# Attention projections emitted one group ahead of the scores, across pairs of heads

## The chip, the cores and the metric

The kernel runs on one core of a Trainium2 chip. The metric is device time in microseconds (us) of one execution, as the median of several runs. Engines are named PE or TensorE (matrix products), DVE or VectorE, ACT or ScalarE, POOL or GpSimd, and SP or SyncE, which here does nothing but issue DMA transfers from one queue, in order.

## What is computed

A trunk of two layers over 1024 tokens of width 1024: a state-space mixer with a feed-forward network, then dilated attention with a second feed-forward network. The change touches the attention only. Cut to what matters, for three groups with dilation 1, 4 and 16 and 16 heads of 64 each:

```python
q = (h @ w_q) * (HEAD_DIM ** -0.5)
for g, (_, dil) in enumerate(DILATED_GROUPS):
    kb, vb = kv_blocks[2 * g], kv_blocks[2 * g + 1]
    qb = _to_residue_blocks(q[:, :, g], dil)
    s = einsum('brnqhe,brnkhe->brnhqk', qb, kb) + bias
    s = where(valid, s, NEG_BIG)
    lse = logsumexp(s)
    p = exp(s - lse)
    outs.append(einsum('brnhqk,brnkhe->brnqhe', p, vb)); lses.append(lse)
wts = softmax(stack(lses), axis=0)
o = einsum('gblh,gblhe->blhe', wts, stack(outs))
return o @ w_out
```

The three groups of a head are merged by one softmax over their sums, so a head's output can begin only when the scores of all three groups are there.

## The kernel before

Products with weights are done in three passes of a split number: a weight tile `raw` (512 KB) is loaded, ScalarE casts it to a high part `wh` (L83), VectorE subtracts for the low part `wl` (L84), and TensorE multiplies `wh`, `wl` with both parts of the activations `hT` (L88 to L90, 24 matmuls for 512 tokens).

The attention works on eight pairs of heads. `values` come first for all heads and are stored to memory. For each pair and each of the groups 0, 1 and 2, `Pair.proj(g)` projects queries and keys: four tiles `qk` of 24 matmuls (two halves of the tokens for queries, two for keys). Each tile is evacuated from PSUM as `qh` (ScalarE, L632 or L635) and `ql` (VectorE, L633 or L636), and small transfers (128 KB, L644 to L647) move them into the stacked tiles `qs` and `kl`, apart for the two heads. `Pair.scores(g)` multiplies queries and keys (L695), VectorE adds the bias tile `bt` and takes the maximum (L683, two instructions), and ScalarE takes exponentials of group 0 (L714). The bias tile of a pair is loaded when the Pair is made (L660, L662). `Pair.output()` loads the values `V` (L810), takes the exponentials of groups 1 and 2 (L740), merges the groups by `softmax()` (two exchange matmuls `x`, L755, each fed by VectorE's `bd`, L750), transposes the weights (`t`, copied to `pt`) and multiplies them with `V` into `o` (L832); VectorE adds the second half of it to `oT` (L876), which is stored as `oscr` (L883).

The pools hold two weight sets, two `raw` tiles, two PSUM banks for `qk`, four for scores, transposes and exchanges together, four `qh`/`ql` tiles, two `V` tiles, one `bt`, and ten `q` tiles for `qs` and `kl`. A group's queries and keys for both heads take six `q` tiles, so group 1's last two tiles (those of the second head's keys) take places that group 0 leaves when its first head is scored.

The kernel doesn't write the order of an engine's instructions. The program's text gives each instruction a priority, and a list scheduler places them by a timing model of its own, with the tiles' dependencies and free buffers. So the emission order shifts priorities, and an engine's queue need not follow it. SyncE's queue gets its transfers in the order that the scheduler fixes, and each waits in it for its own buffers and data.

Of the kernel before, what the change touches and what calls it, by code (L numbers as in the profile page):

```python
# [28 lines left out]
class Pool:  # L29


    def __init__(self, net, pool, bufs):
        self.net, self.pool, self.bufs = net, pool, bufs
# [489 lines left out]
def skew(scr, h0, q0, qstep, nq):  # L523

    ap = scr[:]
    off = ap.offset + h0 * P * LB + q0 * (LB - 1) + 127
    return bass.AP(ap.tensor, off, [[qstep * (LB - 1), nq], [P * LB, 2], [1, 256]])
# [14 lines left out]
def value_tile(net, blk, j, hT, ws, ps, st):  # L542

    nc, g = net.nc, blk // 2
    hf = tile_half(g, j)
    for k in range(KT):
        x = hT[k][hf]
        cols = tok_cols(x, g, j)
        wh, wl = (w[:, (k % 2) * 512 : (k % 2) * 512 + 512] for w in ws[k // 2])
        net.mm3(ps, x[:, 0, cols], x[:, 1, cols], wh, wl, k == 0, k == KT - 1)  # L550
    (nc.scalar.copy if j % 2 else nc.vector.tensor_copy)(st.rearrange("p a b -> p (a b)"), ps)
    h0 = 4 * (blk % 2)
    nc.sync.dma_start(net.vscr[g, h0 : h0 + 4, :, j, :].rearrange("h p c -> p h c"), st)
# [13 lines left out]
def attention(net, hT, ap, ws):  # L567
    nc = net.nc
    net.evn = 0
    for blk in range(2 * NG):  # L570
        if blk:
            ws = [net.wload(net.a["w_v"][blk, i], **({"pool": ap, "tag": "q"} if i < 3 else {})) for i in range(4)]
        else:
            ws = ws + [net.wload(net.a["w_v"][0, i], pool=ap, tag="q") for i in (2, 3)]
        for j in range(8) if blk else range(4, 8):
            ps = net.psA.tile([P, 512], F32, "mm", "v")
            st = ap.tile([P, 4, P], F32, "pt", "vs")
            value_tile(net, blk, j, hT, ws, ps[:], st[:])

    net.oscr = net.dp.tile([8, P, T], F32, name="oscr")  # L580
    nxt = Pair(net, 0, hT, ap)
    nxt.proj(0)
    for hp in range(8):
        pair = nxt
        for g in range(NG):
            if g:
                pair.proj(g)
            pair.scores(g)
        if hp < 7:
            nxt = Pair(net, hp + 1, hT, ap)  # L590
            nxt.proj(0)
        oT = pair.output()

    row = [[net.xp.tile([P, 2, 512], F32R, "x", "gT") for k in range(KT)] for _ in range(2)]
    for k in range(KT):
        if k < 7:
            raw = net.rawp.tile([P, T], F32, "raw", "oraw")
            nc.sync.dma_start(raw[:], net.oscr[k])
        else:
            raw = oT  # L600
        for hf in range(2):
            x = row[hf][k]
            net.split(raw[:, hf * 512 : hf * 512 + 512], x[:, 0, :], x[:, 1, :], nc.gpsimd if k < 7 else nc.vector)
    return [[row[hf][k] for hf in range(2)] for k in range(KT)]
# [46 lines left out]
class Pair:  # L651


    def __init__(self, net, hp, hT, ap):
        nc = net.nc
        self.net, self.hp, self.hT, self.ap = net, hp, hT, ap
        self.qk = {}
        self.bt = ap.tile([P, NG, 2, 256], F32, "bt", "bt")
        for r in range(4):
            nc.sync.dma_start(self.bt[32 * r : 32 * r + 32, 0], skew(net.bscr[0], 2 * hp, r, 4, 32))  # L660
        for g in (1, 2):
            nc.sync.dma_start(self.bt[:, g], skew(net.bscr[g], 2 * hp, 0, 1, P))  # L662
# [858 lines left out]
def program(tc, a, out):  # L1521
    nc = tc.nc
    with ExitStack() as ctx:
# [16 lines left out]
        for l in range(2):  # L1540
            if l == 1:
                with ExitStack() as c:
                    gT = attention(net, hT, setup(net, c), V0)
# [113 lines left out]
```

## Time and profile before

| | |
|---|---|
| time, median of 3 runs | 3102.1 us (3097.02 to 3108.28) |
| the profiled execution's own time | 3093.69 us |
| its span, first to last instruction | 3091.9 us |
| TensorE busy | 2885.9 us (93% of the span) |
| VectorE busy | 1900.4 us (61%) |
| ScalarE busy | 1115.8 us (36%) |
| chain that ended last, share of TensorE | 77% |
| mean granted TensorE clock | 0.962 of full speed |

The profile is one execution. The scores and outputs of the attention lie between about 1400 and 2270 us of the span, and from about 1540 on they repeat with one head pair to a period. Busy shares are means over stages, so the rows further down are taken from this stage alone. A row of a timeline ends, where the engine had been idle, with the idle time in brackets and the operation that ended it.

### The profile page before, as it was taken

How to read it: one execution, taken by the hardware profiler on the slowest of the kernel's cores; microseconds unless marked ns; L12 is line 12 of the kernel's file. 1: busy time of each engine (PE TensorE's matmuls, PEld its weight loads, DVE VectorE, ACT ScalarE, POOL GpSimd, SP SyncE). 2: the span in 40 equal slices, each digit the busy share in tenths (PEclk: the TensorE clock that was granted, in tenths of full speed). 3: DMA queues.
4: the chain of work that ended last, by engine and by line, in shares of the span. 5: the costliest groups of instructions: out<-in, count | busy, mean ns of one | idle time of the engine just before them, and what ended most of it. 6: DMA issues, size and time to landing. Idle time of an engine off the chain costs nothing.

```text
span 3091.9 us, 37869 instructions
## 1 busy us (share of the span) xinstructions
PE 2885.9 (93%) x13926; PEld 2365.8 (77%) x13926; DVE 1900.4 (61%) x3517; ACT 1115.8 (36%) x1939; POOL 260.3 (8%) x259
## 2 busy tenths in 40 slices
PE   3689989999999989999999999999689899999998
PEld 3668768888788868998777777778567688887886
DVE  8964689888666651113544445354457988886577
ACT  2433344444333331103443334343423544443232
POOL 7930000000100000000000000000250000001000
PEclk8889989999999999999999999999799999999999
DMA  5231523333563333326565456456435232336432
GB/s 179 59 119 61 171 86 125 109 109 108 183 255 111 115 121 99 108 72 164 148 153 144 133 133 178 119 150 157 123 141 172 87 123 104 109 106 257 162 134 91
DMA packets 187016, 408.03 MB, mean 132 GB/s; under 512 B 22480, under 2 KB 64192, under 8 KB 186832
## 3 DMA queue, kind: packets, MB, share of 16 engines
q1 hardware_dynamic: 178384, 373.11, 39.0%
q0 software_dynamic: 8448, 32.51, 2.9%
q8 instruction: 110, 1.80, 0.3%
q14 instruction: 74, 0.61, 0.1%
HBM read 249.75 MB, written 89.73 MB: 110 GB/s over the span
## 4 chain that ended last, share of the span: by engine, by line
PE 77%; DVE 6%; issue 6%; POOL 4%; DMA 4%; ACT 2%; SPq 1%; DVEq 0%; POOLq 0%; ACTq 0%
PE dn L412 10%; PE p L89 8%; PE p L90 8%; PE p L88 8%; PE qk L88 6%; PE qk L89 6%; PE qk L90 6%; PE o L832 3%; PE v L88 3%; PE v L90 3%; PE v L89 3%; PE t L822 2%; PE s L695 2%; PE pa L89 1%; PE pa L88 1%
## 5 line engine op out<-in xcount | busy, mean ns | idle before, releaser
L84 DVE TENSOR_TENSOR wl<-raw,wh 128x1024 fp32r<-128x1024 f32 x174 | 222.8, 1281 | 274.3 <-ACT wh L83 270.2
L412 PE MATMUL dn<-wh,ax 128*128 128x512 f32 x1408 | 381.6, 392 | 6.5 <-DVE yv L333 3.9
L88 PE MATMUL p<-xc,wc 128*128 128x512 f32 x880 | 352.1, 401 | 14.2 <-ACT wc L83 14.2
L83 ACT CAST wh<-raw 128x1024 fp32r<-128x1024 f32 x174 | 182.6, 1050 | 495.4 <-PE qk L89 160.5
L89 PE MATMUL p<-xc,wc 128*128 128x512 f32 x880 | 352.2, 400 | 0.0
L90 PE MATMUL p<-xc,wc 128*128 128x512 f32 x880 | 347.9, 400 | 2.7 <-DVE wc L84 2.7
L88 PE MATMUL qk<-hT,wh 128*128 128x512 f32 x768 | 308.9, 402 | 10.4 <-DVE ql L633 10.4
L412 PEld LDWEIGHTS dn<-wh,ax 128*128 128x128 f32 x1408 | 265.7, 189 | 64.2 <-DVE yv L333 4.7
L89 PE MATMUL qk<-hT,wh 128*128 128x512 f32 x768 | 308.7, 402 | 0.0
L90 PE MATMUL qk<-hT,wl 128*128 128x512 f32 x768 | 307.3, 400 | 0.0
L412 PE MATMUL dn<-wl,ax 128*128 128x512 f32 x704 | 218.8, 392 | 0.1
L88 PEld LDWEIGHTS p<-xc,wc 128*128 128x128 f32 x880 | 167.9, 191 | 58.8 <-ACT wc L83 19.2
L90 PEld LDWEIGHTS p<-xc,wc 128*128 128x128 f32 x880 | 167.3, 190 | 44.7 <-DVE wc L84 5.0
L89 PEld LDWEIGHTS p<-xc,wc 128*128 128x128 f32 x880 | 168.0, 191 | 39.4
L83 ACT CAST wc<-s 128x512 fp32r<-128x512 f32 x176 | 107.6, 620 | 239.9 <-PE p L90 158.6
L401 DVE TENSOR_TENSOR wl<-wd,wh 128x1024 fp32r<-128x1024 f32 x88 | 112.8, 1285 | 119.1 <-ACT wh L397 119.0
L88 PEld LDWEIGHTS qk<-hT,wh 128*128 128x128 f32 x768 | 148.0, 193 | 41.8 <-DVE ql L633 12.4
L397 ACT CAST wh<-wd 128x1024 fp32r<-128x1024 f32 x88 | 91.8, 1049 | 228.8 <-PE dn L412 107.8
L90 PEld LDWEIGHTS qk<-hT,wl 128*128 128x128 f32 x768 | 147.9, 193 | 29.7
L89 PEld LDWEIGHTS qk<-hT,wh 128*128 128x128 f32 x768 | 148.1, 193 | 29.0
L88 PE MATMUL v<-wh,hT 128*128 128x512 f32 x384 | 153.7, 401 | 6.7 <-DVE tmp L183 5.5
L683 DVE CUSTOM_DVE_ANT_0 p<-s,bt 128x256 f32<-128x256 f32 (+1 forms) x384 | 119.1, 370 | 65.4 <-PE s L695 64.7
(296 smaller groups left out, 5706.3 us busy)
## 6 DMA issues: line engine op xcount, KB each, us to landing
raw<-in_w_up SPq DMA_DIRECT2D x94, 512.0 KB, 3.6
vs<-cv SPq DMA_DIRECT2D x88, 512.0 KB, 3.0
vs<-vs SPq DMA_DIRECT2D x88, 512.0 KB, 6.3
qs<-qh SPq DMA_DIRECT2D x288, 128.0 KB, 2.4
raw<-in_w_out SPq DMA_DIRECT2D x48, 512.0 KB, 3.5
kl<-ql SPq DMA_DIRECT2D x192, 128.0 KB, 2.4
wd<-in_w_down POOLq DMA_DIRECT2D x44, 512.0 KB, 15.3
raw<-in_w_v SPq DMA_DIRECT2D x26, 512.0 KB, 3.6
```

What stands on the lines that cost most here:

```text
L83: nc.scalar.copy(hi, x)
L84: (eng or nc.vector).tensor_tensor(out=lo, in0=x, in1=hi.bitcast(F32), op=ALU.subtract)
L88: nc.tensor.matmul(out, lh, rh, start=first, stop=False)
L89: nc.tensor.matmul(out, lh, rl, start=False, stop=False)
L90: nc.tensor.matmul(out, ll, rh, start=False, stop=last)
L397: nc.scalar.copy(w[0][:], raw)
L401: nc.vector.tensor_tensor(out=w[1][:], in0=raw, in1=w[0][:].bitcast(F32), op=ALU.subtract)
L412: nc.tensor.matmul(ps[i][h][:], l_, w[wi][:, h * 512 : h * 512 + 512], start=(f == 0 and l_ is ah and wi == 0), stop=(f == NF - 1 and l_ i ...
L683: nc.vector.tensor_tensor_reduce(out=out, in0=s, in1=b, scale=1.0, scalar=-3.0e38, op0=ALU.add, op1=ALU.max, accum_out=m)
L695: nc.tensor.matmul(out, qx[:, qs], kv[i], start=(i == 0), stop=(i == 1))
L822: nc.tensor.transpose(ps[:, i * P : i * P + P], b, net.ident[:])
L832: nc.tensor.matmul(o[64 * h : 64 * h + 64, oc], v[:, 64 * h : 64 * h + 64], pt[h], start=st, stop=sp_)
```

## The change

In the text of the program, the projection of a group is emitted before the scores of the group ahead of it, and the first projection of the next pair before the last scores of this one. For that the load of the bias tile leaves the constructor: it becomes `load_bias()`, called for the next pair after the scores of group 2, since there is one bias tile.

```diff
--- before.py
+++ after.py
@@ -578,17 +578,21 @@
             value_tile(net, blk, j, hT, ws, ps[:], st[:])
 
     net.oscr = net.dp.tile([8, P, T], F32, name="oscr")
+
     nxt = Pair(net, 0, hT, ap)
+    nxt.load_bias()
     nxt.proj(0)
     for hp in range(8):
         pair = nxt
         for g in range(NG):
-            if g:
-                pair.proj(g)
+            if g < 2:
+                pair.proj(g + 1)
+            elif hp < 7:
+                nxt = Pair(net, hp + 1, hT, ap)
+                nxt.proj(0)
             pair.scores(g)
         if hp < 7:
-            nxt = Pair(net, hp + 1, hT, ap)
-            nxt.proj(0)
+            nxt.load_bias()
         oT = pair.output()
 
     row = [[net.xp.tile([P, 2, 512], F32R, "x", "gT") for k in range(KT)] for _ in range(2)]
@@ -652,9 +656,11 @@
 
 
     def __init__(self, net, hp, hT, ap):
-        nc = net.nc
         self.net, self.hp, self.hT, self.ap = net, hp, hT, ap
         self.qk = {}
+
+    def load_bias(self):
+        nc, ap, net, hp = self.net.nc, self.ap, self.net, self.hp
         self.bt = ap.tile([P, NG, 2, 256], F32, "bt", "bt")
         for r in range(4):
             nc.sync.dma_start(self.bt[32 * r : 32 * r + 32, 0], skew(net.bscr[0], 2 * hp, r, 4, 32))
```

What the scheduler makes of it is alike in pairs 1 to 6, and is shown here where the output of pair 1 ends and the scores of pair 2 begin. Lines below L654 of the kernel before are four or six higher in the changed one (L832 is L838 there, L695 is L701).

TensorE, kernel before: the last matmuls of a query projection (`qk_1979`), the last products of the output (`o_1899`), and the first scores of pair 2 (`s_1931` and on).

```order
L90 MATMUL qk_1979_12223<-hT_1416_8397,wl_1973_12185 128x512
L832 MATMUL o_1899_11768<-pt_1917_11850,V_1866_11602 64x256
L695 MATMUL s_1931_11894<-qs_1855_11522,qs_1844_11448 128x128
L695 MATMUL s_1931_11894<-kl_1857_11524,qs_1844_11448 128x128
L695 MATMUL s_1931_11894<-qs_1855_11522,qs_1844_11448 128x256
L832 MATMUL o_1899_11768<-pt_1919_11857,V_1866_11602 64x256
...
L695 MATMUL s_1934_11915<-kl_1857_11524,qs_1844_11448 128x256
L88 MATMUL qk_1979_12223<-hT_1419_8407,wh_1972_12184 128x512
L89 MATMUL qk_1979_12223<-hT_1419_8407,wh_1972_12184 128x512
L90 MATMUL qk_1979_12223<-hT_1419_8407,wl_1973_12185 128x512
L695 MATMUL s_1936_11932<-qs_1856_11523,qs_1845_11449 128x128
```

TensorE in the changed kernel, the same place (`qk_1973` is the same query projection).

```order
L88 MATMUL qk_1973_12169<-hT_1419_8407,wh_1966_12130 128x512
L89 MATMUL qk_1973_12169<-hT_1419_8407,wh_1966_12130 128x512
L90 MATMUL qk_1973_12169<-hT_1419_8407,wl_1967_12131 128x512
L838 MATMUL o_1899_11768<-pt_1917_11850,V_1866_11602 64x256
L701 MATMUL s_1955_12052<-qs_1848_11461,qs_1837_11387 128x128
L701 MATMUL s_1955_12052<-kl_1850_11463,qs_1837_11387 128x128
...
L838 MATMUL o_1899_11768<-pt_1921_11868,V_1867_11604 64x128
L838 MATMUL o_1899_11768<-pt_1923_11875,V_1867_11604 64x128
L701 MATMUL s_1958_12073<-qs_1848_11461,qs_1837_11387 128x256
L701 MATMUL s_1958_12073<-kl_1850_11463,qs_1837_11387 128x256
```

The query projection's last three matmuls stood behind the output and between the scores of the two heads; now they stand ahead of both. Three score matmuls stood ahead of the last output product (`o_1899`); now twelve do.

SyncE's queue, kernel before: the next two value tiles, the store of the output, the keys of group 1 of pair 2 for the second head (eight transfers of `qs_1956` and `kl_1958`), and the query weights `raw_2102` of group 1 of pair 3.

```order
L75 DMA raw_2013_12475<-in_w_k 128x1024
L810 DMA V_2026_12559<-vscr_8203 128x1024
L810 DMA V_2027_12561<-vscr_8203 128x1024
L883 DMA oscr_9803<-oT_1898_11766 128x1024
L646 DMA qs_1956_12051<-qh_1960_12079 64x512
L647 DMA kl_1958_12053<-ql_1961_12080 64x512
L646 DMA qs_1956_12051<-qh_1960_12079 64x512
...
L647 DMA kl_1958_12053<-ql_1964_12117 64x512
L75 DMA raw_2102_12929<-in_w_q 128x1024
```

SyncE's queue in the changed kernel (`raw_2085` are the same weights, `qs_1939` and `kl_1941` the same keys).

```order
L816 DMA V_1867_11604<-vscr_8203 128x1024
L75 DMA raw_2085_12846<-in_w_q 128x1024
L816 DMA V_2026_12559<-vscr_8203 128x1024
L816 DMA V_2027_12561<-vscr_8203 128x1024
L650 DMA qs_1939_11968<-qh_1943_11996 64x512
L651 DMA kl_1941_11970<-ql_1944_11997 64x512
L889 DMA oscr_9803<-oT_1898_11766 128x1024
L650 DMA qs_1939_11968<-qh_1943_11996 64x512
L651 DMA kl_1941_11970<-ql_1944_11997 64x512
...
L651 DMA kl_1941_11970<-ql_1947_12034 64x512
```

The weight load stood behind the eight key transfers and now stands ahead of the two value tiles; the output's store moved behind the first two key transfers.

VectorE, kernel before: the output's add (`oT_1898`), the first adds of bias to scores (`p1_1924`) and the split of a weight tile (`wl_2004`, whose `raw` the load above replaces).

```order
L825 COPY pt_1923_11875<-t_1922_11870 128x512
L876 TENSOR_TENSOR oT_1898_11766<-oT_1898_11766,o_1899_11768 128x1024
L683 ISA p1_1924_11887,st1_1928_11891<-s_1931_11894,bt_1840_11435 128x128
...
L683 ISA p1_1925_11888,st1_1928_11891<-s_1936_11932,bt_1840_11435 128x256
L683 ISA st1_1928_11891 128x1
L84 TENSOR_TENSOR wl_2004_12404<-raw_2002_12401,wh_2003_12403 128x1024
```

VectorE in the changed kernel.

```order
L831 COPY pt_1923_11875<-t_1922_11870 128x512
L689 ISA p1_1948_12045,st1_1952_12049<-s_1955_12052,bt_1864_11593 128x128
L689 ISA st1_1952_12049 128x1
L689 ISA p1_1948_12045,st1_1952_12049<-s_1955_12052,bt_1864_11593 128x256
L689 ISA st1_1952_12049 128x1
L84 TENSOR_TENSOR wl_1997_12343<-raw_1995_12340,wh_1996_12342 128x1024
...
L689 ISA p1_1948_12045,st1_1952_12049<-s_1957_12066,bt_1864_11593 128x256
L689 ISA st1_1952_12049 128x1
L882 TENSOR_TENSOR oT_1898_11766<-oT_1898_11766,o_1899_11768 128x1024
L689 ISA p1_1948_12045,st1_1952_12049<-s_1958_12073,bt_1864_11593 128x256
```

The split stood behind the output's add and ten adds; now it stands behind two adds, and six adds stand ahead of the output's add.

On ScalarE, the first evacuation `qh` of group 2's queries stood between the exponentials of group 0 for the first head and those for the second; now it stands behind both, next to the second evacuation.

## Rows read from the trace of the kernel before

**Rows 1.** Busy time by 100 us: span, PE, PEld, DVE, ACT, POOL, clock, DMA share, GB/s.

```profile
1600.00:1700.00 100.00, 96.11 (x527) 76.54 (x527) 40.51 (x145) 39.05 (x98) 0.00 (x0) 0.95 0.53 141
```

**Rows 2.** Waits of TensorE, 1400 to 2230: us in total, times, longest.

```profile
PE s L695 <- DMA qs<-qh: 13.1, 13, 3.4
...
PE qk L88 <- DVE ql L633: 10.4, 7, 1.5
```

**Rows 3.** Timeline of TensorE where it waited: start, us, idle before it.

```profile
1547.62 0.79 PE L88 MATMUL qk<-hT,wh 128*128 128x512 f32 x1 [1.47 <-DVE ql L633]
...
1649.43 0.30 PE L695 MATMUL s<-qs,qs 128*128 128x128 f32 x1 [1.37 <-DMA qs<-qh]
...
1651.68 0.55 PE L695 MATMUL s<-qs,qs 128*128 128x256 f32 x1 [0.24 <-DMA qs<-qh]
...
1655.33 0.79 PE L88 MATMUL qk<-hT,wh 128*128 128x512 f32 x1 [1.47 <-DVE ql L633]
...
2194.08 0.79 PE L88 MATMUL qk<-hT,wh 128*128 128x512 f32 x1 [1.52 <-DVE ql L633]
```

**Rows 4.** Timeline of TensorE, its pace in scores and in projections.

```profile
1640.46 0.28 PE L695 MATMUL s<-kl,qs 128*128 128x256 f32 x1
...
1641.54 0.28 PE L695 MATMUL s<-qs,qs 128*128 128x256 f32 x1
...
1661.13 0.39 PE L88 MATMUL qk<-hT,wh 128*128 128x512 f32 x1
...
1661.82 0.39 PE L88 MATMUL qk<-hT,wh 128*128 128x512 f32 x1
```

**Rows 5.** Timeline of SyncE's DMA queue, 1640 to 1649: start, us.

```profile
1640.00 0.81 SPq L810 DMA_DIRECT2D V<-vscr  x2
...
1641.54 0.32 SPq L883 DMA_DIRECT2D oscr<-oT  x1
1641.95 0.47 SPq L646 DMA_DIRECT2D qs<-qh  x1
...
1647.85 0.59 SPq L647 DMA_DIRECT2D kl<-ql  x1
1648.54 0.53 SPq L75 DMA_DIRECT2D raw<-in_w_q  x1
```

**Rows 6.** Busy time by 2 us, columns as in rows 1.

```profile
1638.00:1640.00 2.00, 2.00 (x25) 1.60 (x23) 0.00 (x0) 0.00 (x0) 0.00 (x0) 1.00 0.00 0
...
1642.00:1644.00 2.00, 2.00 (x15) 1.76 (x13) 2.00 (x13) 1.05 (x1) 0.00 (x0) 1.00 0.91 309
1644.00:1646.00 2.00, 1.86 (x15) 1.54 (x13) 2.00 (x8) 0.00 (x0) 0.00 (x0) 1.00 1.00 362
...
1648.00:1650.00 2.00, 0.57 (x4) 0.39 (x3) 2.00 (x16) 2.00 (x11) 0.00 (x0) 0.99 1.07 225
1650.00:1652.00 2.00, 1.76 (x8) 1.54 (x8) 0.79 (x7) 2.00 (x9) 0.00 (x0) 0.50 0.90 272
```

**Rows 7.** Timeline of VectorE at the same place.

```profile
1640.30 1.22 DVE L876 TENSOR_TENSOR oT<-oT,o 128x1024 f32<-128x1024 f32 x1 [5.60 <-PE o L832]
...
1641.64 0.42 DVE L683 CUSTOM_DVE_ANT_0 p<-s,bt 128x256 f32<-128x256 f32 x1
...
1644.61 1.22 DVE L84 TENSOR_TENSOR wl<-raw,wh 128x1024 fp32r<-128x1024 f32 x1
...
1654.59 1.48 DVE L633 TENSOR_TENSOR ql<-qk,qh 128x512 fp32r<-128x512 f32 x2
```

**Rows 8.** Timeline of ScalarE at the same place.

```profile
1646.63 0.40 ACT L714 ACTIVATE p<-p,nm 128x128 f32<-128x128 f32 x1 [3.15 <-DVE nm L711]
...
1650.48 0.57 ACT L632 CAST qh<-qk 128x512 fp32r<-128x512 f32 x1
```

**Rows 9.** Timeline of all engines, 1693 to 1699, at the exchange matmul.

```profile
1693.38 0.29 DVE L750 TENSOR_TENSOR bd<-st,mask 128x128 f32<-128x128 f32 x1
...
1698.50 0.38 PE L755 MATMUL x<-bd,eye 128*128 128x128 f32 x2
```

## Prediction

> **What bounds the kernel now.** I read the table by 100 us stretches first, then who waited for whom on TensorE in the attention stage, then the timeline of one waiting place on TensorE, the DMA queue, VectorE and ScalarE. In the attention stage TensorE is the bound: a typical 100 us has it 96.11 us busy [rows 1]. It waits at one place in each head pair, and the reader is to see how it repeats: after the scores of groups 0 and 1, the first matmul of the key projection of group 2 is held back 1.47 to 1.52 us at 1547.62, 1655.33 and 2194.08, seven times in all, about 108 us apart [rows 3]. Over the stage the two large waits there are 13.1 us for the transfers `qs<-qh` and 10.4 us for `ql` [rows 2].
>
> One such place, from 1640 to 1656, gives the chain. The keys of group 1 for the second head need eight transfers of 128 KB, which need buffers that group 0 frees when its first head's scores are done. The DMA queue issues two V loads at 1640.00, the store of the output at 1641.54, then these eight from 1641.95 to 1647.85 [rows 5]. The DMA engines are full all this time (busy share 0.91 and 1.00, 309 and 362 GB/s, then 225 GB/s) [rows 6]. TensorE starts the second head's scores at 1649.43, waits again, and goes on at 1651.68, when the second half of the keys has landed [rows 3]. VectorE follows with the adds and then makes `ql` of the query projection at 1654.59, which frees a PSUM bank, and the projection resumes at 1655.33 [rows 3, 7]. So the chain is: V loads, output store, eight key transfers, last scores, adds, `ql`, resume. It takes 11.7 us from the first V load to 1651.68 and 3.65 us from there to the resume, the latter partly at half clock (0.50 in the row of 1650) [rows 3, 5, 6].
>
> **The change part by part.** No instruction's work is added or removed: the same 288 projection matmuls and the same scores per pair. The scheduler already took next-pair projections ahead before, so emission order changes priorities, and the printed order is what counts. In six of the seven places it is alike in every pair.
>
> *Where the projections stand.* Scores of group 2 now come after whole projection tiles, and the filler around them moves. All of this lies in stretches without a named wait, so I cost it at nothing. Its cover is thinnest before the first exchange matmul `x`: VectorE had its input at 1693.38 and TensorE reached it at 1698.50, 4.8 us after the 0.29 us operation ended [rows 9]. Now 48 projection matmuls stand between the last scores and `x` where 64 stood; at 0.23 us each (three steps from 1661.13 to 1661.82 [rows 4]) that takes 3.7 us off, so about 1.1 us of cover is left.
>
> *The waiting place itself.* Groups 0 and 1 are still scored one behind the other, 64 matmuls with no projection between (before, three stood inside). The wait is not filled. What moves is the chain's head. First, the last three projection matmuls (0.69 us) and nine more score matmuls (1.08 us from 1640.46 to 1641.54 [rows 4]) now come before the last output matmul, which the V loads wait for: they issue about 1.75 us later, near 1641.75. Second, on the DMA queue the load of the next weights (512 KB), which went out at 1648.54 behind all eight key transfers [rows 5], now stands ahead of these V loads. It waits for VectorE's weight split, which comes after two adds; VectorE, which sat idle 5.60 us before the output's add [rows 7], gets there early: first scores done about 1638.5, two adds 0.8 us, split 1.22 us [rows 7], so the load goes out near 1640.75. Third, the output's store moves behind the first two key transfers, still ahead of six.
>
> So ahead of the last key transfers now lie four transfers of 512 KB and not three. One costs 524 KB / 309 to 362 GB/s = 1.45 to 1.7 us [rows 6]. The chain is then 11.7 + 1.5 = 13.2 us from 1640.75: 1653.95, which is 2.3 us late. If the early load hid completely, it is 1641.75 + 11.7 = 1653.45, 1.8 us late. I take 2.0 us. What is late next: last scores, adds, `ql` and the projection, one for one, since nothing else is queued that TensorE could take. In the seventh place no weights are left to load and only the 1.75 us apply; I count it as 2.0 too. Sum: 7 x 2.0 = 14 us. Bounds for one place: 0.75 us, if only the DMA queue's issue counts (the last key transfer at about 1648.6 for 1647.85), and 3.0 us, if the load starts late and the clock's low stretch grows with the wait.
>
> [...]
>
> *ScalarE.* Before, the evacuation `qh` ran at 1650.48, between the exponentials of the two heads; it now stands behind both. Exponentials of one head take 3.85 us (1646.63 to 1650.48) [rows 8]. VectorE's lead brings the first to about 1646.1: 1646.1 + 7.7 + 0.57 for `qh` + 0.7 for `ql` [rows 7, 8] = 1655.1, against the 1655.33 of now. This chain neither gains nor loses, and the key transfers decide.
>
> *The tail.* Five and not three of the stored outputs are read back behind the last projection. Those reads and splits run beside the last softmax; I cost them at nothing. In front of the last output matmuls they could cost some 4 us, and the weight casts that leave that stretch could give 1 us back.
>
> The profiled execution took 3093.69 us, 8.4 us under the median of 3102.1. The sum against its own time: 3093.7 + 14 = 3107.7. On the median: 3116.
>
> **Rivals.**
> 1. *Chain late, as above*: slower by 5 to 21 us (seven times 0.75 to 3.0). For it: full DMA engines in rows 6, and scores that visibly wait for these transfers in rows 3. Chance 0.52; time 3116.
> 2. *The change does not do what it says.* The order at the waiting place was already that of a projection ahead, the wait stays, and the early weight load fits into DMA time that is idle anyway, as it is from 1638 to 1640 [rows 6]. Then ScalarE's chain sets the resume, within 0.2 us of now: 3102, give or take the 5 us by which runs differ. For it: most of the program's order is the same. Against: the V loads hang on the last output matmul, which the order puts later. Chance 0.26.
> 3. *VectorE's lead wins (faster).* The first adds no longer stand behind the output's add, so VectorE starts at about 1638.8 for 1640.30, 1.4 us ahead. If the last keys land before about 1650.3, adds, exponentials and `ql` all move up: 7 x 1.4 = 10 us, 3092. It decides at that landing; the full DMA engines speak against it. Chance 0.09.
> 4. *The cover before `x` breaks.* Exponentials or the weight split end over 1.1 us later than I count, and TensorE waits at `x` or at the first output matmuls besides: 2 us more in six pairs, 12 us on top of case 1, 3128. For it: a split of 1.22 us [rows 7] now stands on VectorE between the last adds and the maximum that the exponentials need. Against: I already count it. Chance 0.13.
>
> **How the numbers follow.** I forecast case 1, 3116 us. About 0.3% (9.3 us) is what a measurement of this kernel tells from no change. Of case 1 some four fifths lie above that (0.42), with case 4 0.55 slower. Same: the rest of case 1 and most of case 2, 0.34. Faster: case 3 and a little of case 2, 0.11. The range leaves out case 3's better half and the ends of 4: 3096 to 3133; case 1 alone would be 3107 to 3123.
>
> **What would show it.** In the changed kernel's trace: the weight load issued ahead of two V loads, these at about 1.7 us later against the scores; the second head's second `qs` wait ending 2 us later against the first scores of group 0; resume after a `ql` wait about 110 us apart and not 108; no wait at `x` in pairs 0 to 6. The forecast is wrong if the weight load goes out more than 2 us before the V loads (then its bytes cost nothing), if the period stays at 108 us, or if TensorE finds projections to do inside the 64 scores.

## The result and the profile after

The changed kernel takes 3123.73 us (median of 4 runs, 3122.29 to 3128.43) against 3099.56 us for the kernel before in the same comparison: ratio 1.0077, 95% interval 1.0059 to 1.0096. It is about 24 us slower; 14 us had been forecast. The profiled execution has a span of 3121.9 us, a clock of 0.959.

A place, below, is the waiting place of one head pair; its resume is the first projection matmul that TensorE does behind the second head's scores; a period goes from one resume to the next. Up to the sixth resume TensorE has done the same matmuls in either kernel, so what is lost there is idle time and slower work.

Of the 30.0 us between the two profiled spans, 7.6 us lie ahead of the stage that the change touches: at 1400 us the changed kernel has 33 fewer projection matmuls behind it (33 x 0.23 us), in code that is the same. That is a difference of two executions and not the change's. Up to the first resume another 4.9 us are lost (1560.13 for 1547.62, less 7.6), in the five periods that follow 22.2 us (561.94 for 539.78 between the first resume and the sixth). From there to the exchange matmul of the last pair 0.5 us come back, and 4.1 us from there to the end. So six places lose 27 us, 4.4 us each in those five periods, and the seventh and the tail give some back.

The table by 100 us has TensorE 93.01 us busy, where it was 96.11 us [rows 1]:

```profile
1600.00:1700.00 100.00, 93.01 (x504) 73.56 (x503) 42.97 (x147) 34.78 (x83) 0.00 (x0) 0.93 0.52 137
```

The waits of TensorE between 1400 and 2230, which answer to [rows 2]:

```profile
PE s L701 <- DMA qs<-qh: 33.9, 6, 6.4
PE qk L88 <- DVE ql L637: 9.1, 6, 1.5
PE s L701 <- DMA kl<-ql: 7.0, 2, 6.8
```

The wait for the transfers has grown, that for `ql` is what it was. There is no wait for `x` in pairs 0 to 6. TensorE's timeline at the waits, for [rows 3]:

```profile
1560.13 0.80 PE L88 MATMUL qk<-hT,wh 128*128 128x512 f32 x1 [1.52 <-DVE ql L637]
...
1665.75 0.45 PE L701 MATMUL s<-qs,qs 128*128 128x128 f32 x1 [5.47 <-DMA qs<-qh]
...
1671.19 0.80 PE L88 MATMUL qk<-hT,wh 128*128 128x512 f32 x1 [1.52 <-DVE ql L637]
...
2122.07 0.80 PE L88 MATMUL qk<-hT,wh 128*128 128x512 f32 x1 [1.52 <-DVE ql L637]
```

Several short waits have become one of 5.47 us ahead of the second head's scores. The DMA queue at this place, for [rows 5]:

```profile
1653.73 0.33 SPq L75 DMA_DIRECT2D raw<-in_w_q  x1
1655.42 0.80 SPq L816 DMA_DIRECT2D V<-vscr  x2
1656.32 0.47 SPq L650 DMA_DIRECT2D qs<-qh  x1
1656.88 0.55 SPq L651 DMA_DIRECT2D kl<-ql  x1
1657.52 0.54 SPq L889 DMA_DIRECT2D oscr<-oT  x1
...
1663.90 0.60 SPq L651 DMA_DIRECT2D kl<-ql  x1
```

This is the order that was forecast: weight load, V loads, two key transfers, store, six key transfers. VectorE and ScalarE there, for [rows 7, 8]:

```profile
1667.89 0.29 DVE L689 CUSTOM_DVE_ANT_0 p<-s,bt 128x128 f32<-128x128 f32 x1 [5.34 <-PE s L701]
...
1670.44 1.28 DVE L637 TENSOR_TENSOR ql<-qk,qh 128x512 fp32r<-128x512 f32 x2
```

```profile
1659.61 0.40 ACT L720 ACTIVATE p<-p,nm 128x128 f32<-128x128 f32 x1 [8.10 <-DVE nm L717]
...
1667.27 1.05 ACT L636 CAST qh<-qk 128x512 fp32r<-128x512 f32 x2
```

VectorE stands 5.34 us idle until the scores come, and `ql` follows the last add. The clock there, by 2 us as in [rows 6]:

```profile
1662.00:1664.00 2.00, 0.00 (x0) 0.00 (x0) 0.55 (x5) 2.00 (x10) 0.00 (x0) 0.66 1.02 345
...
1674.00:1676.00 2.00, 2.00 (x6) 1.58 (x5) 0.00 (x0) 0.00 (x0) 0.00 (x0) 0.50 0.88 204
1676.00:1678.00 2.00, 2.00 (x9) 1.63 (x8) 0.00 (x0) 0.00 (x0) 0.00 (x0) 0.93 0.04 10
```

The granted clock goes to 0.50 in the wait and is still 0.50 for 5.1 us after the resume. Over the places, windows of 1 us put 13.7 us at 0.50 in each of the places 2 to 6 after the change, and 6.8 or 10.2 us (mean 8.9) before it.

To compare kernels I cut a period in two: from a resume to the issue of the next two V loads, and from these to the next resume. The numbers are means over the places 2 to 6, worked out from the timelines of TensorE and the DMA queue. Ratios are to the kernel before, with the 95% interval; the first column of times is the median. Where projections stand among the second head's scores (experiments 6 to 8) or the V loads behind the keys, there is nothing to cut by; in experiments 6 and 7 the period is that of the first projection matmul behind the scores of group 0. Each number is from one profiled execution; the scale of chance is seen from experiment 4, which has the changed kernel's order at these places and differs from it by 0.13 us to the V loads, 0.33 us from them, and 0.20 us in the period.

| kernel | us | ratio | period | to V loads | from V loads |
|---|---|---|---|---|---|
| before | 3099.6 to 3106.6 | 1 | 107.96 | 92.94 | 15.02 |
| after | 3123.73 | 1.0077 (1.0059 to 1.0096) | 112.39 | 96.04 | 16.35 |
| 1 weight load and evacuation back | 3097.35 | 0.9981 (0.9968 to 0.9994) | 108.79 | 94.91 | 13.88 |
| 2 V loads back | 3086.18 | 0.9944 (0.9922 to 0.9967) | 105.83 | - | - |
| 3 both loads back | 3086.14 | 0.9946 (0.9929 to 0.9962) | 105.71 | - | - |
| 4 across pairs only | 3120.19 | 1.0060 (1.0038 to 1.0082) | 112.59 | 95.91 | 16.68 |
| 5 evacuation early | 3103.29 | 0.9999 (0.9987 to 1.0011) | 109.64 | 94.47 | 15.17 |
| 6 within the pair only | 3034.57 | 0.9769 (0.9743 to 0.9796) | 99.59 | - | - |
| 7 within, V loads back | 3030.97 | 0.9758 (0.9740 to 0.9776) | 99.24 | - | - |
| 8 key tile first | 3096.59 | 0.9970 (0.9959 to 0.9981) | 107.18 | - | - |
| 9 weight load alone | 3122.87 | 1.0059 (1.0039 to 1.0078) | 111.13 | 95.76 | 15.37 |
| 10 output first | 3093.35 | 0.9960 (0.9946 to 0.9974) | 107.54 | 92.35 | 15.19 |
| 11 before, evacuation early | 3080.98 | 0.9922 (0.9902 to 0.9942) | 105.94 | 92.45 | 13.49 |
| 12 weight load and output | 3115.23 | 1.0024 (1.0009 to 1.0039) | 109.33 | 93.74 | 15.59 |

The kernel before read 3099.6 us with the first comparison and up to 3106.6 us later, so ratios are to be compared, not medians.

### The profile page after: what moved, and what is told of

It reads as the page before. It is cut to its first block, busy times and chain, and to the rows that moved or that the text cites. A ratio compares the mean times of both kernels' runs of the same rounds, so it can differ in the third digit from the quotient of the medians.

```text
span 3121.9 us, 37873 instructions
## 1 busy us (share of the span) xinstructions
PE 2889.6 (93%) x13926; PEld 2371.2 (76%) x13926; DVE 1899.4 (61%) x3517; ACT 1116.4 (36%) x1939; POOL 260.6 (8%) x259
## 4 chain that ended last, share of the span: by engine, by line
PE 81%; DVE 6%; DMA 5%; POOL 4%; ACT 1%; issue 1%; SPq 1%; DVEq 0%; ACTq 0%; POOLq 0%
PE dn L412 15%; PE p L88 7%; PE p L89 7%; PE p L90 7%; PE qk L88 6%; PE qk L89 6%; PE qk L90 6%; PE o L838 3%; PE v L88 3%; PE v L90 3%; PE v L89 3%; PE t L828 2%; PE s L701 2%; DMA qs<-qh 1%; PE pa L89 1%; PE pa L88 1%
## 5 line engine op out<-in xcount | busy, mean ns | idle before, releaser
L397 ACT CAST wh<-wd 128x1024 fp32r<-128x1024 f32 x88 | 91.8, 1050 | 232.9 <-issue 108.4
```

The source lines that it names most:

```text
L397: nc.scalar.copy(w[0][:], raw)
```

## The experiments

**1. The weight load behind the key transfers.** A dependency of issue order alone is added for the one weight load of each pair that the change put ahead of the V loads.

```diff
-        nc.sync.dma_start(raw[:], src)
+        with self.tc.issue_after(after.ins) if after else nullcontext():
+            nc.sync.dma_start(raw[:], src)
...
-            proj(net, net.wload(net.a[w][hp, g]), self.hT, g, w == "w_q", self.ap) for w in ("w_q", "w_k")
+            proj(net, net.wload(net.a[w][hp, g], after=self.prev if g == 1 and w == "w_q" else None), self.hT, g, w == "w_q", self.ap) for w in ("w_q", "w_k")
```

> The weight load goes behind the eight key transfers again, as it stood before the change; the order of TensorE's matmuls is that of the changed kernel in every pair, and on VectorE one `ql` moves up between the adds of the two heads. Theory A (the chain is late because 512 KB of weights move ahead of the keys): the second head's scores start 10.3 - 1.5 = 8.8 us after the V loads, 1.5 us x 6 places = 9 us less, 3115 us. Theory B (only the later release of the V loads counts, since they wait for the last output matmul with or without the weight load): the second head still starts about 10.3 us after the V loads and the time stays at 3124 us, or falls by at most 6 x 1.5 = 9 us through the `ql` wait alone, to be seen as a wait for `ql` that is gone. Theory C (it is TensorE's own order, not the queue): 3124 us.

Measured: 3097.35 us, by the ratios 30 us below the changed kernel and more than theory A could give. The way from the V loads to the resume is 2.5 us shorter, and the wait for `ql` is gone but for one place. The scheduler had moved the evacuation as well (`qh` between the two heads' exponentials, `ql` among the adds), so this run mixes two causes. Experiments 5 and 9 take them apart.

**2 and 3. The V loads behind the key transfers, without and with the weight load.**

```diff
-            nc.sync.dma_start(v[:], net.vscr[g, self.hp])
+            with net.tc.issue_after(self.key1.ins) if g < 2 and self.hp else nullcontext():
+                nc.sync.dma_start(v[:], net.vscr[g, self.hp])
```

> The two V loads of each pair go behind the eight key transfers; the weight load stays ahead of these; TensorE's order is that of the changed kernel in every pair. Theory A: of the three loads ahead of the keys one is left, so the keys land 2 x 1.5 = 3 us earlier, 6 x 3 = 18 us less: 3106 us. Theory B (the release of the V loads is what is late): the keys no longer hang on the last output matmul at all but on the first head's scores, so the whole 4.4 us a place comes back, 6 x 4.4 = 26 us: 3097 us. Theory C: 3124 us.

> Weight load and V loads both behind the eight key transfers, TensorE's order that of the changed kernel. Theory A: 3 x 1.5 = 4.5 us a place, 6 x 4.5 = 27 us less: 3097 us. Theory B: as with the V loads alone, 3097 us. Theory C: 3124 us, with second-head waits of 5.5 us or more as now.

Measured: 3086.18 and 3086.14 us, faster than either theory gave. The period falls to 105.83 and 105.71 us, under that of the kernel before. TensorE's order is the changed kernel's, so theory C (that order alone) is out. Its waits for the keys fall from 5.5 to 6.8 us a place to 1.8 to 2.9 us: what stands ahead of the keys in this queue sets when the second head's scores can start, and with the V loads gone the weight load makes no difference any more. `qh` and `ql` moved up here too, so the full 6.6 us a place aren't the V loads' alone.

**4. The part across pairs alone.**

```diff
-            if g < 2:
-                pair.proj(g + 1)
-            elif hp < 7:
+            if g:
+                pair.proj(g)
+            if g == 2 and hp < 7:
```

> Only the part of the change across pairs: the first projection of the next pair ahead of the scores of group 2, while groups 1 and 2 of the same pair are projected ahead of their own scores as before. The order on TensorE comes out as that of the changed kernel in pairs 1 to 7. Every theory that blames this order or the queue says 3124 us; if the part within the pair mattered by itself, the time would come out near 3100 us or differ by over 5 us.

Measured: 3120.19 us and a period of 112.59 us, the changed kernel's. From the first resume to the sixth its order is the changed kernel's on every engine, so this part alone brings the order that loses.

**5. The evacuation early, weight load still ahead.** The exponentials of the second head are set behind `qh`, its last four adds behind `ql`.

```diff
+            for e in self.late:
+                net.tc.add_manual_dep(e.ins, self.first[0].ins.name, NOSYNC, reason="qh first")
...
+                        with net.tc.issue_after(self.first[1].ins) if g == 1 and h else nullcontext():
+                          ttr(p4[h][:, r, g * 256 : g * 256 + 256], ps[:, t * 256 : t * 256 + 256], bt[:, g, h, :], mg[:, g - 1, h, 2 * r + 1 : 2 * r + 2])
```

> The changed kernel with its weight load still ahead of the V loads; only the evacuation of the first query projection of group 2 is moved ahead: on ScalarE `qh` before the second head's exponentials, on VectorE `ql` before the last four adds. TensorE's order is unchanged in pairs 1 to 6. It takes the gain of putting the weight load back (3.7 us a place) apart. If the transfer's 512 KB are the cause, the second head still starts 10.3 to 11.8 us after the V loads, the wait for `ql` of 1.52 us goes, and 6 x 1.5 = 9 us come back: 3115 us. If the late evacuation is the cause (ScalarE's order, which the prediction costed at nothing), nearly all of it comes back: 3124 - 6 x 3.7 = 3102 us.

Measured: 3103.29 us, ratio 0.9999: the loss is made up, as the second theory had it. ScalarE's timeline of this kernel:

```profile
1654.30 0.41 ACT L727 ACTIVATE p<-p,nm 128x128 f32<-128x128 f32 x1 [8.10 <-DVE nm L724]
1660.64 0.58 ACT L636 CAST qh<-qk 128x512 fp32r<-128x512 f32 x1 [2.40 <-DMA kl<-ql]
```

`qh` waits 2.40 us for the key transfers, which still read the buffers that it wants to write. But that the gain is as large as the loss does not make the late evacuation its cause: before the change `ql` stood behind the adds as well [rows 7]. Experiment 11 asks this.

**11. The kernel before with its evacuation early.** The same dependency on the last four adds; `qh` stood between the heads' exponentials already.

```diff
+            for e in self.late:
+                net.tc.add_manual_dep(e.ins, net.first[1].ins.name, NOSYNC, reason="ql first")
```

> The kernel before the change, with `ql` of group 2 ahead of the last four adds of the second head, as in the fifth experiment. If the change lost its time because it put the evacuation late, the kernel before has nothing to get back here: 3104 us as before. If the wait for `ql` (1.47 us in each place of before too) is a cost of both kernels that the change did not bring, it goes here as well: 7 x 1.47 = 10 us and up to 10 more by a shorter half-clock stretch, 3084 to 3094 us.

Measured: 3080.98 us, ratio 0.9922. Moving the evacuation takes 0.78% off the kernel before and 0.78% (1.0077 to 0.9999) off the kernel after, each to within about 0.2%. It is a cost of both, which the change did not bring.

**9. The weight load alone.** As experiment 1, with `qh` and `ql` held where the changed kernel has them.

```diff
+            net.tc.add_manual_dep(self.first[0].ins, self.late.ins.name, NOSYNC, reason="qh last")
...
+                if g == 1 and h:
+                    net.tc.add_manual_dep(self.first[1].ins, e.ins.name, NOSYNC, reason="ql last")
```

> The weight load behind the eight key transfers as in the first experiment, but with `qh` and `ql` of group 2 held where the changed kernel has them (behind the second head's exponentials and adds), so that the load alone is moved. If the load's bytes are worth what the first experiment showed between V loads and second head (10.95 to 9.75 us), 1.2 us a place come back, 6 x 1.2 = 7 us, and up to 1 us more a place by a shorter half-clock stretch: 3111 to 3117 us. If they were worth nothing and all came from the evacuation's place: 3124 us. If they were all: 3097 us.

Measured: 3122.87 us, ratio 1.0059. Its interval overlaps that of the change, so the times alone don't show a gain. The trace does: from the first resume to the sixth nothing but the load has moved, and the period is 1.26 us shorter. Of this, 0.98 us lie behind the V loads and show in each of the five places (0.6 to 1.6 us); the other 0.28 us change sign from place to place and are not shown. This was predicted in kind, and it is the smaller part.

One reason why the times don't show it lies in pair 0, where the hold on `qh` and `ql` applies as well. From the first projection matmul of the stage to the first V load (1525.40) this kernel takes 141.8 us and the changed one 135.4 us, with a wait for `ql` of 3.41 us that neither main kernel has. Experiment 12 has the same wait (141.5 us). The periods, taken from the first resume on, don't contain it.

**10. The last output matmuls ahead of all but two scores.**

```diff
-                nc.tensor.matmul(out, qx[:, qs], kv[i], start=(i == 0), stop=(i == 1))
+                with net.tc.issue_after(net.lastpv.ins) if g == 0 and h == 0 and self.hp and qs.start > 0 else nullcontext():
+                    nc.tensor.matmul(out, qx[:, qs], kv[i], start=(i == 0), stop=(i == 1))
```

> The changed kernel, but only two scores and not twelve stand ahead of the last output matmuls, which the V loads wait for; nothing else moves. If the V loads' release sets the end of the chain, it comes 10 x 0.12 = 1.2 us earlier, and up to 1.8 us since the output's matmuls are no longer broken up by scores: 6 x 1.2 to 1.8 = 7 to 11 us back, 3113 to 3117 us. If the key transfers hang on the first head's scores instead, which are as late as before: 3124 us.

Measured: 3093.35 us, by the ratios 36 us below the changed kernel, where 7 to 11 us were expected. More had moved than I wrote there: the scheduler put the weight load behind the V loads and `ql` among the adds. The part that the edit was made for shows in the way to the V loads: 92.35 for 96.04 us.

**12. Weight load and output together, the evacuation held late.** The edits of 9 and 10.

> Weight load behind the key transfers, last output matmuls ahead of all but two scores, evacuation held late: the two causes that the prediction named for the later chain undone together, with the changed kernel's projections where they are. If these two are the loss, the time is that of before, 3100 to 3107 us (the sum of what the two give alone). If more than 8 us of the 24 are left, something else of the changed order costs.

Measured: 3115.23 us, ratio 1.0024; a period of 109.33 us. The causes named in the prediction, undone together, give back 3.06 of the 4.43 us a place: 1.26 for the load (experiment 9), 1.80 for the output matmuls (from 9 to 12). With these the output's add and its store have moved ahead again, too, so 1.80 us is for all three. 1.37 us a place are left, some 8 us; the time is 7 us above the kernel before, but about 6 us of that are pair 0's, as in experiment 9. How much of the loss stays unexplained is thus known only roughly.

**6 and 7. The part within the pair alone, without and with the V loads behind the keys.**

```diff
             if g < 2:
                 pair.proj(g + 1)
-            elif hp < 7:
-                nxt = Pair(net, hp + 1, hT, ap)
-                nxt.proj(0)
             pair.scores(g)
         if hp < 7:
+            nxt = Pair(net, hp + 1, hT, ap)
             nxt.load_bias()
+            nxt.proj(0)
```

> Only the part of the change within a pair (groups 1 and 2 are projected ahead of the scores of the group before; the next pair's first projection and its bias stay behind the scores of group 2). Here the printed order puts 21 projection matmuls between the two heads' scores of group 0, 16 more ahead of those of group 1 and the whole first key tile of group 2 inside these: 37 x 0.23 = 8.5 us of cover that the key transfers have not had. If the stall is a matter of cover, both its parts go, the 4.3 us of named waits a place of before and about half of its 9.1 us at half clock: 7 x 6 to 8.5 = 42 to 60 us, 3045 to 3060 us. Rival: the key tile of group 2 then stands first in line and waits for its PSUM bank, whose evacuation needs buffers that the key transfers hold: a wait for `ql` of 2 to 4 us takes the old one's place, 3080 us.

> The part within a pair alone, with the two V loads behind the eight key transfers. If what is left of the stall there hangs on these transfers, 1 to 2 us a place less than without: 7 to 14 us. If the cover already hides them, the same time within 5 us.

Measured: 3034.57 and 3030.97 us, 2.3% and 2.4% faster than the kernel before, below even the range I gave. The table by 100 us of experiment 6:

```profile
1600.00:1700.00 100.00, 100.00 (x571) 80.40 (x569) 48.53 (x175) 41.63 (x102) 0.00 (x0) 1.00 0.61 157
```

TensorE is busy for all of these 100 us, at a granted clock of 1.00. The same queue, in the same order as before the change (V loads, store, keys), is now covered; the DMA queue, and then TensorE:

```profile
1625.09 0.81 SPq L815 DMA_DIRECT2D V<-vscr  x2
1626.57 0.32 SPq L888 DMA_DIRECT2D oscr<-oT  x1
...
1633.37 0.46 SPq L650 DMA_DIRECT2D kl<-ql  x1
```

```profile
1633.44 0.28 PE L700 MATMUL s<-kl,qs 128*128 128x256 f32 x1
1633.56 0.39 PE L90 MATMUL qk<-hT,wl 128*128 128x512 f32 x1
...
1637.00 0.39 PE L90 MATMUL qk<-hT,wl 128*128 128x512 f32 x1
1637.23 0.22 PE L700 MATMUL s<-qs,qs 128*128 128x128 f32 x1
...
1638.60 0.28 PE L700 MATMUL s<-qs,qs 128*128 128x256 f32 x1
1638.72 0.39 PE L88 MATMUL qk<-hT,wh 128*128 128x512 f32 x1
```

These 16 matmuls of the second query tile of group 2 stand between the scores of groups 0 and 1, and a whole key tile begins inside those of group 1. The V loads come 99.2 us after those of the pair before (1724.31 is next), where they took 108.4 us before the change (1748.41 after 1640.00). With the V loads out of the way nothing more is gained for certain (the intervals overlap).

**8. A projection really ahead of the scores that wait.** On top of 3 and 5, the second head's scores of group 1 are set behind the first key tile of group 2.

```diff
-                nc.tensor.matmul(out, qx[:, qs], kv[i], start=(i == 0), stop=(i == 1))
+                with net.tc.issue_after(self.fill.ins) if g == 1 and h else nullcontext():
+                    nc.tensor.matmul(out, qx[:, qs], kv[i], start=(i == 0), stop=(i == 1))
```

> The changed kernel with the weight load and the V loads behind the key transfers, the evacuation early, and the second head's scores of group 1 set behind the first key tile of group 2, so that a projection really stands ahead of the scores that wait. Against the 3086 us of both loads back: if the bank comes free before the keys land, up to the 1.2 to 2.8 us of named wait and part of the 6.8 us of half clock a place go, 7 x 3 = 21 us, 3065 us. If the bank itself waits for the key transfers (the evacuation needs their buffers), nothing is gained: 3086 us, with a wait for `ql` where the scores' wait was.

Measured: 3096.59 us, by the ratios 7 us worse than experiment 3, where the second case had it level; the wait for `ql` came as that case had it. The waits of TensorE, 1400 to 2230:

```profile
PE qk L89 <- DVE ql L640: 25.3, 11, 3.7
```

The key tile has no free bank: `ql` frees it, behind `qh`. In three of the seven places `qh` waits 8.4 us for a key transfer (at 1654.45, for one), whose buffers it is to write; in the other four it stands behind the first head's exponentials. So that tile doesn't cover these transfers here; in experiment 6 the tiles that do are those which still have a bank. Much of the order around it moved as well, so its price is not taken apart.

## Why the prediction was right, and where its sizes were off

*The waiting place is not filled: right.* The wait is still there and has grown, and the projection still follows the scores. Experiments 4 and 6 and their orders say why. Projecting the next pair ahead of the scores of group 2 uses the projections up earlier in the pair, and at the waiting place only the tile without a bank is left; without that part, two tiles are left to stand among these scores. The prediction weighed the change as one order, and did not see that one half of it alone is worth 2.3%.

*V loads later by 1.75 us: right in kind, mis-sized.* They are issued 3.10 us later after the resume (96.04 for 92.94). The same stretch by windows, from the first of the last output matmuls to the V loads, of the kernel before and of the one after:

```profile
1637.12:1640.00 2.88, 2.88 (x28) 2.10 (x27) 0.00 (x0) 0.00 (x0) 0.00 (x0) 1.00 0.00 0
```

```profile
1650.59:1655.42 4.83, 4.83 (x37) 3.28 (x36) 3.34 (x14) 0.92 (x1) 0.00 (x0) 1.00 0.13 21
```

Nine more matmuls cost 1.95 us and not 1.08: scores and outputs break each other's runs. Around such a change of kind the next matmul starts 0.21 to 0.23 us later (1653.05 for 1652.82, 1653.49 for 1653.28), where it is 0.12 us among scores:

```profile
1652.82 0.39 PE L701 MATMUL s<-qs,qs 128*128 128x256 f32 x1
1653.05 0.28 PE L701 MATMUL s<-kl,qs 128*128 128x256 f32 x1
1653.16 0.28 PE L701 MATMUL s<-qs,qs 128*128 128x256 f32 x1
1653.28 0.28 PE L701 MATMUL s<-kl,qs 128*128 128x256 f32 x1
1653.49 0.43 PE L838 MATMUL o<-pt,V 128*64 128x128 f32 x2
```

Experiment 12, with ten of the scores out of there again, has its V loads 2.02 us earlier than experiment 9 (93.74 for 95.76). The three projection matmuls come to 0.7 to 0.9 us. About 0.3 us are left. The clock can cost as much, by an estimate: behind a resume it is 0.50 for 5.1 us on average and not 4.6 us (places 1 to 5), and projection matmuls start 0.43 us apart there (1671.78 to 1676.05, ten steps), for 0.23 us at 1.00.

*The early weight load and the store: right in kind, mis-sized.* The way from the V loads to the resume was to grow by some 0.25 us (2.0 in all, less 1.75); it grew by 1.33 us, 0.98 us of it through the load (experiment 9). The key transfers show it. Issues and their median time to landing, before (1639 to 1650) and after (1653 to 1666):

```profile
qs<-qh SPq DMA_DIRECT2D x4, 128.0 KB, 5.2
kl<-ql SPq DMA_DIRECT2D x4, 128.0 KB, 4.7
```

```profile
qs<-qh SPq DMA_DIRECT2D x4, 128.0 KB, 6.9
kl<-ql SPq DMA_DIRECT2D x4, 128.0 KB, 6.3
```

For one such load the prediction had estimated 1.45 to 1.7 us from the rates of [rows 6]. The trace of experiment 9 has 0.98 us behind the V loads and 1.26 us in the period; it times a place and not the transfer, so what the bytes alone cost is not shown.

*The sum.* The step "I take 2.0 us" is the term that was off: 4.43 us a place, outside the bounds of 0.75 to 3.0. Of it, 1.26 us are the load, 1.80 the output matmuls behind more scores (with the output's add and store), and 1.37 are left, of which the three projection matmuls, by their length alone, explain 0.7 to 0.9; the rest stays open. Counted by idle time instead, the waits of the timeline over 0.35 us add up to 45.1 us in the places 1 to 6 after the change and to 21.0 us before it, 4.0 us a place more.

That the time still lies inside the range of 3096 to 3133 us is in part luck. Case 1 alone, with at most 3.0 us a place, was to end at 3123; the range reached further for rival 4, which did not come. And what was too small for a place was partly made good by counting seven places, where six show in the end.

*Seven places: six.* The last place lost 2.6 us (109.30 us from the sixth resume to the seventh, 106.68 before), and got them back ahead of the exchange matmul behind it, where TensorE waits for the exponentials in either kernel (10.8 us now, 11.5 before): 141.04 us from the sixth resume to that matmul, 141.57 before. 6 x 4.4 = 27 us less 0.5.

*ScalarE neither gains nor loses: right for the change.* `qh` ends at 1668.3, and `ql` begins at 1670.44, behind the last add. But experiments 5 and 11 show that the order around it, which I took for given in "last scores, adds, `ql`", is worth 0.78% in both kernels.

*The cover before `x`, and the tail:* the first held (no wait for `x` in pairs 0 to 6), the second came out 4 us shorter and not level, which may be no more than the two executions' difference: from the last V load to the end the changed kernel takes 832.6 us, experiment 4 829.8 us, the kernel before 835.9 us. Rival 4 did not come; rival 3 neither, as VectorE's first adds do start ahead of the output's add (1651.92 for 1655.65) and then stand idle for the keys. Rival 2, that the load hides, is out by the trace of experiment 9, though not by its time. Of the signs that were named, the weight load does go out ahead of the V loads, by 1.69 us (1653.73, 1655.42), and the period is 112.4 us where 110 was said.

## What to carry to other kernels

Work emitted further ahead was not more cover here: it was spent earlier, and at a wait only what is left in line counts. So look in the printed order at which independent tiles, with free PSUM banks of their own, stand between the issue of the transfers and the matmul that needs them. When a change has two halves, time each alone; here they have opposite signs (-2.3% and +0.6%), and together the worse one wins. When an ordering edit gains, read what else the scheduler moved, and try the same edit on the kernel before: a gain as large as the loss need not be its cause.

## What the runs showed of the hardware

Scores set among the output's matmuls cost TensorE more time than in a run of their own, though it was never idle there (2.88 us busy of 2.88 before, 4.83 of 4.83 after): 1.95 us for nine scores, which take 1.08 us in a run, and 2.02 us for ten (from experiment 9 to 12).

Transfers stood waiting at the head of the DMA queue, some of them, by the profile's attribution, for an earlier load to land. The queue's own waits of the changed kernel, 1400 to 2230:

```profile
SPq L75 <- DVE wl L84: 108.5, 6, 18.1
...
SPq L650 <- DMA V<-vscr: 7.7, 6, 1.8
```

The weight load waits up to 18.1 us at the head for its buffer, and a key transfer, as the profile attributes it, up to 1.8 us for a V load with which it shares no data. Whether it was that load that held it back, no run shows, nor which part of the 6.3 to 6.9 us to landing is due to what.

In experiment 6, with no idle time from 1600 to 1700, the granted clock was 1.00 there; the changed kernel has 0.93 to 0.99 in its rows by 100 us from 1500 to 2200. The period is 99.59 us in experiment 6, 8.4 us less than before. Of the period before, 3.5 us were waits (21.0 / 6), and the 8.9 us at 0.50 cost up to 4.4 us more, an estimate that takes half of them.
